# A two-layer fp32 decoder trunk on one core: half of each MLP's first matrix by Strassen's seven products

## The chip, the core and the metric

The kernel runs on one core of a Trainium2 chip. Its engines work at the same time and meet through semaphores: TensorE (PE; its loads of the stationary operand are listed as PEld), VectorE (DVE), ScalarE (ACT), and SyncE (SP), which here only issues DMAs. Each engine takes its instructions in the order in which they stand in the built program. The metric is the device time of one execution in microseconds (us); lower is better.

## The reference

The input has 256 tokens of 2048 features in float32, and everything is computed to float32 accuracy. Layer 0 is differential attention and an MLP, layer 1 a Mamba-2 mixer and an MLP. Only the two MLPs matter here (D_FF is 8192):

```python
def rms_norm(x, gain):
    xf = x.astype(jnp.float32)
    y = xf * lax.rsqrt(jnp.mean(xf * xf, axis=-1, keepdims=True) + EPS)
    return (y * gain.astype(jnp.float32)).astype(x.dtype)
...
def sq_relu_mlp(h, w1, w2):
    return jnp.square(jax.nn.relu(h @ w1)) @ w2
...
        h = h + mix.astype(h.dtype)
        h = h + sq_relu_mlp(rms_norm(h, mlp_norm[i]), mlp_w1[i], mlp_w2[i]).astype(h.dtype)
```

## The kernel before

**Products in two halves.** TensorE multiplies in a rounded type (fp32r). So each float32 operand is split into a high part (ACT's cast) and a low part (what is left, DVE's subtraction), and a product is high x high + low x high + high x low. Weights come from memory as units of 128 x 1024 (512 KB), one DMA each on SP's queue into the tile raw (6 buffers, `load`, L169). `split_weights` (L147) makes wh on ACT (L152) and wl on DVE (L153), with 4 buffers each.

**Two forms of a product.** In the *wide* form (`sub_block`, L156) a 128 x 128 block of weights is stationary, and the activations of all 256 tokens move past it, high and low side by side: 512 columns for wh (L162) and 256 columns for wl (L166). A unit is 8 blocks, so 8 + 8 matmuls. The result stands with features on partitions. In the *token* form (`token_block`, L202) 128 tokens of an activation are stationary and 512 weights move. A unit is 12 matmuls of 512 columns (L216, L218), and the result stands with tokens on partitions.

**The MLP** (`mlp`, L475) goes in four quarters q of 2048 hidden features. A quarter has two stages. The first (W1) makes 16 hidden blocks of 128 features in 8 calls of `wide_pair` (L180), 4 units each. Behind each call `add_sums` (L196) brings the two halves of a PSUM bank together (ACT copy L199, DVE add L200), L485 makes the squared ReLU, and `split_pair` (L227) makes high and low parts (L230, L231). The second (W2) multiplies these with four column blocks of the second matrix (`token_block`, 8 units each), and L490 adds the result, scaled by the token's norm, to h. The eight input tiles xs of the first quarter come from `norm_input` (L250): TensorE transposes h (L259), and `x_parts` (L235) scales and splits (L240 on ACT, L241 on DVE). They are made while the last quarter of the attention's (or the mixer's) output matrix is still being multiplied; `residual` (L282) updates h there (L284).

**Order.** The Python code writes instructions in a nominal order. Generators in `side` are advanced at fixed places (`side.tick()`) and put small work between the matmuls. Behind that a scheduler of the build puts each engine's instructions into their final order. PSUM has 8 banks: 4 for pp (L96), 4 for small results (L97, tags aux and aux1).

Of the kernel before, what the change touches and what calls it, by code (L numbers as in the profile page):

```python
# [12 lines left out]
F32 = mybir.dt.float32  # L13
# [75 lines left out]
def trunk_kernel(ctx: ExitStack, tc: tile.TileContext, x, xt, par, rope, qk, wv, wo, w10, w20, win, wdt, wout, w11, w21, out):  # L89
# [6 lines left out]
    ps = ctx.enter_context(tc.tile_pool(name="ps_mm", bufs=4, space=PSUM))  # L96
    ps_ax = ctx.enter_context(tc.tile_pool(name="ps_ax", bufs=3, space=PSUM))  # L97
# [71 lines left out]
    def load(src, n=1):  # L169

        raw = wp.tile([P, 1024], F32, tag="raw", bufs=6, name="raw")
        w = 1024 // n
        for i in range(n):
            nc.sync.dma_start(out=raw[:, i * w:(i + 1) * w], in_=src[:, i * w:(i + 1) * w])
        return raw

    def bank():
        return ps.tile([P, 2, T], F32, tag="mm", name="pp")
# [23 lines left out]
    def token_block(src, j, acts):  # L202

        pp = [bank().rearrange("p a b -> p (a b)") for _ in range(2)]
        n = src.shape[0]
        for s in range(n):
            w = split_weights(load(src[s, j]))
# [13 lines left out]
        return pp  # L221

# [64 lines left out]

    xs = []
# [23 lines left out]
    with tc.tile_pool(name="att", bufs=1) as ap:  # L312
# [139 lines left out]
        for hd in range(NH):  # L452
# [20 lines left out]


    def mlp(xs, w1, w2, pool, after):  # L475
        r2 = const.tile([P, 2], F32, tag="r2", bufs=2, name="r2")
        for q in range(4):
            hid = []
            for j in range(8):
                r = pool.tile([P, 2, T], F32, tag="relu", bufs=2, name="relu")  # L480
                add_sums(r, wide_pair(w1, 16 * q + 2 * j, xs))
                if q == 0 and j == 1:
                    norm_mean()
                    V.reciprocal(out=r2, in_=ms)
                V.scalar_tensor_tensor(out=r, in0=r, scalar=0.0, in1=r, op0=ALU.max, op1=ALU.mult)  # L485
                hid += split_pair(r)
            for j in range(4):
                pp = token_block(w2[8 * q:8 * q + 8], j, hid)
# [270 lines left out]
def _blocks(w, order=None):  # L759
# [5 lines left out]
    return _units(b)  # L765

# [71 lines left out]
```

## Time and profile before

| What | us |
| --- | --- |
| median of 3 runs (2512.38 to 2512.57) | 2512.4 |
| the profiled execution's own time | 2510.96 |
| its span (first to last instruction) | 2509.2 |
| PE busy in the span | 2493.1 |
| DVE busy | 1668.7 |
| ACT busy | 1310.0 |

The busy time of an engine is the time in which at least one of its instructions ran. Instructions that follow each other overlap a little at their ends, on PE by almost half of a short one: what a chain of them costs is read from the distance of their starts and not from one's duration. A stretch of the span with the engines' busy times in it shows which of them has room there.

### The profile page before, as it was taken

How to read it: one execution, taken by the hardware profiler on the slowest of the kernel's cores; microseconds unless marked ns; L12 is line 12 of the kernel's file. 1: busy time of each engine (PE TensorE's matmuls, PEld its weight loads, DVE VectorE, ACT ScalarE, POOL GpSimd, SP SyncE). 2: the span in 40 equal slices, each digit the busy share in tenths (PEclk: the TensorE clock that was granted, in tenths of full speed). 3: DMA queues.
4: the chain of work that ended last, by engine and by line, in shares of the span. 5: the costliest groups of instructions: out<-in, count | busy, mean ns of one | idle time of the engine just before them, and what ended most of it. 6: DMA issues, size and time to landing. Idle time of an engine off the chain costs nothing.

```text
span 2509.2 us, 33804 instructions
## 1 busy us (share of the span) xinstructions
PE 2493.1 (99%) x13038; PEld 2122.0 (85%) x13038; DVE 1668.7 (67%) x2158; ACT 1310.0 (52%) x1919; POOL 1.2 (0%) x8
## 2 busy tenths in 40 slices
PE   8999999999999999999999999999999999999999
PEld 6888888888888888888888888888888888888887
DVE  7888876655555556558886887887665565555554
ACT  6656655434434434456776575674544443443443
POOL 0000000000000000000000000000000000000000
PEclk9999999999999999999999999999999999999999
DMA  8445555555555565556655556455555555656564
GB/s 276 163 157 181 167 176 183 187 193 193 187 193 191 187 199 187 190 179 207 196 186 195 175 188 207 159 186 187 184 190 193 192 186 193 193 188 193 189 197 139
DMA packets 131122, 471.26 MB, mean 188 GB/s; under 512 B 14640, under 2 KB 14832, under 8 KB 130960
## 3 DMA queue, kind: packets, MB, share of 16 engines
q1 hardware_dynamic: 127152, 458.28, 56.1%
q10 hardware_dynamic: 3808, 10.81, 1.3%
q8 instruction: 102, 1.67, 0.3%
q14 instruction: 60, 0.49, 0.1%
HBM read 466.88 MB, written 2.16 MB: 187 GB/s over the span
## 4 chain that ended last, share of the span: by engine, by line
PE 99%; DMA 1%; SPq 0%; issue 0%; DVE 0%; ACT 0%; DVEq 0%
PE pp L162 35%; PE pp L216 28%; PE pp L166 18%; PE pp L218 14%; PE aux L650 1%; PE aux L135 0%; PE aux L397 0%; PE aux L259 0%; DMA raw<-in_qk 0%; PE aux L620 0%; PE aux L651 0%; PE aux L426 0%; DMA xf<-in_x 0%; PE aux L427 0%; PE aux L607 0%; PE aux L420 0%
## 5 line engine op out<-in xcount | busy, mean ns | idle before, releaser
L153 DVE TENSOR_TENSOR wl<-raw,wh 128x1024 fp32r<-128x1024 f32 (+1 forms) x867 | 1057.2, 1222 | 711.0 <-ACT wh L152 704.8
L152 ACT CAST wh<-raw 128x1024 fp32r<-128x1024 f32 (+1 forms) x867 | 908.1, 1049 | 1074.1 <-PE pp L218 507.0
L162 PE MATMUL pp<-act,wh 128*128 128x512 f32 x3856 | 979.3, 394 | 11.8 <-DVE act L241 11.8
L162 PEld LDWEIGHTS pp<-act,wh 128*128 128x128 f32 x3856 | 693.0, 189 | 138.1 <-ACT wh L152 11.1
L216 PE MATMUL pp<-wh,act 128*128 128x512 f32 x1536 | 601.3, 391 | 0.0
L218 PE MATMUL pp<-wh,act 128*128 128x512 f32 x1536 | 599.0, 390 | 0.0
L166 PEld LDWEIGHTS pp<-act,wl 128*128 128x128 f32 x3856 | 524.6, 191 | 37.7 <-issue 1.7
L166 PE MATMUL pp<-act,wl 128*128 128x256 f32 x3856 | 540.8, 283 | 0.0
L216 PE MATMUL pp<-wl,act 128*128 128x512 f32 x1536 | 413.4, 391 | 0.0
L216 PEld LDWEIGHTS pp<-wh,act 128*128 128x128 f32 x1536 | 288.5, 188 | 60.2 <-issue 1.0
L218 PEld LDWEIGHTS pp<-wh,act 128*128 128x128 f32 x1536 | 288.8, 188 | 58.1
L216 PEld LDWEIGHTS pp<-wl,act 128*128 128x128 f32 x1536 | 286.6, 188 | 59.9 <-issue 1.0
L575 DVE SCALAR_TENSOR_TENSOR cy<-u,cwb,cy 128x256 f32<-128x256 f32 x144 | 62.5, 480 | 21.3 <-ACT cy L573 21.2
L490 DVE SCALAR_TENSOR_TENSOR h<-pp,r,h 128x512 f32<-128x512 f32 x64 | 45.1, 747 | 43.0 <-PE pp L216 43.0
L200 DVE TENSOR_TENSOR relu<-pp,relu 128x256 f32<-128x256 f32 x128 | 53.5, 418 | 0.0
L199 ACT COPY relu<-pp 128x256 f32<-128x256 f32 x128 | 46.9, 367 | 0.0
L485 DVE SCALAR_TENSOR_TENSOR relu<-relu 128x512 f32<-128x512 f32 x64 | 44.3, 692 | 2.2
L635 ACT ACTIVATE m<-ab,acol 128x128 f32<-128x128 f32 x128 | 41.6, 391 | 6.7 <-PE aux L651 6.7
L284 DVE TENSOR_TENSOR h<-pp,h 128x512 f32<-128x512 f32 x48 | 31.0, 685 | 19.7 <-PE pp L216 19.7
L231 DVE TENSOR_TENSOR act<-relu,act 128x512 fp32r<-128x512 f32 x64 | 43.9, 686 | 0.0
L230 ACT CAST act<-relu 128x512 fp32r<-128x512 f32 x64 | 39.2, 613 | 0.0
L240 ACT ACTIVATE act<-aux,pa 128x256 fp32r<-128x256 f32 x48 | 21.6, 472 | 12.4 <-DVE act L241 9.4
(175 smaller groups left out, 954.0 us busy)
## 6 DMA issues: line engine op xcount, KB each, us to landing
raw<-in_w SPq DMA_DIRECT2D x512, 512.0 KB, 4.0
raw<-in_win SPq DMA_DIRECT2D x160, 512.0 KB, 3.5
raw<-in_wout SPq DMA_DIRECT2D x64, 512.0 KB, 3.5
raw<-in_qk SPq DMA_DIRECT2D x63, 512.0 KB, 4.2
raw<-in_wv SPq DMA_DIRECT2D x32, 512.0 KB, 3.3
raw<-in_wo SPq DMA_DIRECT2D x32, 512.0 KB, 3.5
ab<-dram_a ACTq DMA_DIRECT2D x16, 512.0 KB, 5.1
xf<-in_x SPq DMA_DIRECT2D x8, 256.0 KB, 6.6
```

Of the source, the lines that this page charges most:

```text
L152: S.copy(out=wh[:, s], in_=raw[:, s])
L153: V.tensor_tensor(out=wl[:, s], in0=raw[:, s], in1=wh[:, s].bitcast(F32), op=ALU.subtract)
L162: PE.matmul(acc, lhsT=wh[:, k * P:(k + 1) * P], rhs=acts[k0 + k], start=(start and k == 0), stop=False)
L166: PE.matmul(acc[:, 0, :], lhsT=wl[:, k * P:(k + 1) * P], rhs=acts[k0 + k][:, 0, :], start=False, stop=(stop and k == 7))
L199: S.copy(out=dst[:, t, :], in_=pp[t][:, 1, :])
L200: V.tensor_tensor(out=dst[:, t, :], in0=pp[t][:, 0, :], in1=dst[:, t, :], op=ALU.add)
L216: PE.matmul(pp[t], lhsT=act[:, 0, tok], rhs=m, start=(s + i + k == 0), stop=(s == n - 1 and i + k == 2))
L218: PE.matmul(pp[t], lhsT=act[:, 1, tok], rhs=m, start=False, stop=False)
L231: V.tensor_tensor(out=t[:, :, 1, :], in0=src, in1=t[:, :, 0, :].bitcast(F32), op=ALU.subtract)
L485: V.scalar_tensor_tensor(out=r, in0=r, scalar=0.0, in1=r, op0=ALU.max, op1=ALU.mult)
L490: V.scalar_tensor_tensor(out=h[:, t, cols(j)], in0=pp[t], scalar=r2[:, t:t + 1], in1=h[:, t, cols(j)], op0=ALU.mult, op1=ALU.add)
L575: V.scalar_tensor_tensor(out=y[:, i, :], in0=u[:, i, k:k + T], scalar=cwb[:, w + k:w + k + 1], in1=y[:, i, :], op0=ALU.mult, op1=ALU.add)
```

## The change

In each quarter, half of the first matrix (8 of the 16 hidden blocks, 1024 features) is multiplied in the token form by Strassen's method in Winograd's variant. Tokens, inner dimension and features are each cut in two, and the 8 products of the halves become 7 products of sums. The other half stays in the wide form.

- `seven` handles 256 of the 2048 inner features. It loads four weight blocks of 128 x 512 (1 MB, two DMAs L513 and L514, into the tile raw7 with 2 buffers), makes three sums of them on DVE (L529, two blocks in one instruction of 1024; L531 and L532, 512 each), splits all seven blocks (three casts and subtractions of 1024 and one of 512, L522 and L523), and issues 7 x 3 matmuls of 512 columns (L536 to L538) into seven PSUM banks, in which the eight calls of a quarter add up. `seven_out` combines the seven banks into the four results (one ACT copy, seven DVE operations of 512).
- `sum_parts` makes the four sums of activations for each pair of inner blocks, once per MLP: two additions of 256, four operations of 128 and a split of 512 on DVE (L492 to L503).
- `hidden` takes the squared ReLU of the result (L569, one DVE instruction of 2048), transposes it on TensorE (16 transposes of 128 x 128 per quarter, L576) and splits it as before (L240). The W2 stage takes the wide form's hidden blocks first.
- In the nominal order a call of `seven` and a `wide_one` (two units) alternate; in the first quarter two `wide_one` stand ahead, and two calls of `seven` stand alone at the end.
- During an MLP all 8 PSUM banks are one pool (7 + 1 in a W1 stage); elsewhere the pools are as before. The weights' high and low parts share a tile w of 4 buffers; raw has 4 buffers instead of 6. The square's unused output is bf16.

The host lays the Strassen half of the weights out as four blocks per call; it does no sums.

```diff
-        wh = wp.tile([P, 1024], F32R, tag="wh", bufs=4, name="wh")
-        wl = wp.tile([P, 1024], F32R, tag="wl", bufs=4, name="wl")
+        w = wp.tile([P, 2, 1024], F32R, tag="w", bufs=4, name="w")
+        wh, wl = w[:, 0, :], w[:, 1, :]
...
-        raw = wp.tile([P, 1024], F32, tag="raw", bufs=6, name="raw")
+        raw = wp.tile([P, 1024], F32, tag="raw", bufs=4, name="raw")
...
+    def seven(pool, src, acts, pp, start, stop):
+        r = pool.tile([P, 7, NB], F32, tag="raw7", bufs=2, name="raw7")
+        nc.sync.dma_start(out=r[:, 0:3, :], in_=src[:, 0:3, :])
+        nc.sync.dma_start(out=r[:, 6, :], in_=src[:, 3, :])
...
+        parts(0, 2)
+
+        V.tensor_tensor(out=r[:, 3:5, :], in0=r[:, 0:2, :], in1=bc(r[:, 6, :], 2), op=ALU.subtract)
+        parts(2, 2)
+        V.tensor_tensor(out=r[:, 5, :], in0=r[:, 1, :], in1=r[:, 3, :], op=ALU.add)
+        V.tensor_tensor(out=r[:, 6, :], in0=r[:, 5, :], in1=r[:, 2, :], op=ALU.subtract)
+        parts(4, 2)
+        parts(6, 1)
+        for n, ((ah, al), (wh, wl)) in enumerate(zip(acts, ws)):
+            PE.matmul(pp[n], lhsT=ah, rhs=wh, start=start, stop=False)
+            PE.matmul(pp[n], lhsT=al, rhs=wh, start=False, stop=False)
+            PE.matmul(pp[n], lhsT=ah, rhs=wl, start=False, stop=stop)
...
+        def hidden(u, hid):
+            V.scalar_tensor_tensor(out=u, in0=u, scalar=0.0, in1=u, op0=ALU.max, op1=ALU.mult)
+            yield from wait(2)
...
+                        PE.transpose(ax[:, f, t * P:(t + 1) * P], uf[:, t, T * j + P * f:T * j + P * f + P], ident)
+                hid += split_pair(ax)
...
-            for j in range(8):
-                r = pool.tile([P, 2, T], F32, tag="relu", bufs=2, name="relu")
-                add_sums(r, wide_pair(w1, 16 * q + 2 * j, xs))
...
+            for j in range(8 + wait_for):
+                if j >= wait_for:
...
+                    seven(pool, w1s[q, i], sas[i], p7, i == 0, i == 7)
+                    if i == 7:
+                        u = seven_out(pool, p7)
+                if j < 8:
...
+                    add_sums(r[:, j % 2:j % 2 + 1], [wide_one(w1, 8 * q + j, xs)])
```

**PE in a W1 stage.** Before, units of the wide form follow each other (two of them here):

```order
L162 MATMUL pp<-act,wh 128x512 x8
L166 MATMUL pp<-act,wl 128x256 x8
L162 MATMUL pp<-act,wh 128x512 x8
L166 MATMUL pp<-act,wl 128x256 x8
L162 MATMUL pp<-act,wh 128x512 x8
```

After, in the second quarter, two wide units (L168 and L172 are their lines now) and then the products of a call of `seven`, three matmuls each; sa is a sum of activations:

```order
L168 MATMUL pp<-act,w 128x512 x8
L172 MATMUL pp<-act,w 128x256 x8
L168 MATMUL pp<-act,w 128x512 x8
L172 MATMUL pp<-act,w 128x256 x8
L536 MATMUL pp<-w,act 128x512
L537 MATMUL pp<-w,act 128x512
L538 MATMUL pp<-w,act 128x512
L536 MATMUL pp<-w,sa 128x512
L537 MATMUL pp<-w,sa 128x512
L538 MATMUL pp<-w,sa 128x512
L536 MATMUL pp<-w,act 128x512
```

What moved: where four wide units stood, there are now two, and 21 matmuls of the token form.

**DVE in a W1 stage.** Before, one call of `wide_pair` (four splits):

```order
L153 TENSOR_TENSOR wl<-raw,wh 128x1024
L231 TENSOR_TENSOR act<-relu,act 128x2x256
L153 TENSOR_TENSOR wl<-raw,wh 128x1024 x2
L200 TENSOR_TENSOR relu<-pp,relu 128x256
L153 TENSOR_TENSOR wl<-raw,wh 128x1024
L200 TENSOR_TENSOR relu<-pp,relu 128x256
L485 SCALAR_TENSOR_TENSOR relu<-relu 128x512
```

After, one step of the second quarter, from one add of a wide block's halves (L206) to the next; raw_5402 and raw_5490 are the weights of this call of `seven` and of the next:

```order
L206 TENSOR_TENSOR relu<-pp,relu 128x256
L603 SCALAR_TENSOR_TENSOR relu<-relu 128x512
L159 TENSOR_TENSOR w<-raw,w 128x1024 x2
L240 TENSOR_TENSOR act<-relu,act 128x2x256
L523 TENSOR_TENSOR w<-raw_5402,w 128x1024 x2
L529 TENSOR_TENSOR raw_5490<-raw_5490 128x1024
L531 TENSOR_TENSOR raw_5490<-raw_5490 128x512
L532 TENSOR_TENSOR raw_5490<-raw_5490 128x512
L523 TENSOR_TENSOR w<-raw_5402,w 128x1024
L523 TENSOR_TENSOR w_5505<-raw_5490,w_5505 128x512
L206 TENSOR_TENSOR relu<-pp,relu 128x256
```

What moved: the next call's sums (L529 to L532) stand among this call's splits. In every second step L603 and L240 are absent, since a squared ReLU takes two wide blocks, and one more L523 stands behind L529 and not ahead of it.

**DVE where the first quarter begins.** Before, the last update of h and the last input tiles, close together:

```order
L284 TENSOR_TENSOR h<-pp,h 128x512 x2
L153 TENSOR_TENSOR wl<-raw,wh 128x1024
L279 TENSOR_REDUCE ms<-ssq 128x2
L280 TENSOR_SCALAR ms<-ms 128x2
L484 RECIPROCAL r_3841<-ms 128x2
L153 TENSOR_TENSOR wl<-raw,wh 128x1024
L241 SCALAR_TENSOR_TENSOR act<-aux,pa,act 128x256 x4
```

After, the end of that stretch (the update of h stands ten rows ahead of it); L250 is the input tile's low part, L492 to L503 are sums of activations, and L523 is the first split of the first call of `seven`:

```order
L602 RECIPROCAL r_3718<-ms 128x2
L492 TENSOR_TENSOR a<-act 128x256 x2
L250 SCALAR_TENSOR_TENSOR act<-aux,pa,act 128x256
L503 TENSOR_TENSOR sa<-asum,sa 128x512
L496 TENSOR_TENSOR asum<-a 128x128
L523 TENSOR_TENSOR w<-raw_3892,w 128x1024
L250 SCALAR_TENSOR_TENSOR act<-aux,pa,act 128x256 x2
L497 TENSOR_TENSOR asum<-asum,a 128x128
L498 TENSOR_TENSOR asum<-a 128x128
L499 TENSOR_TENSOR asum<-a,asum 128x128
L250 SCALAR_TENSOR_TENSOR act<-aux,pa,act 128x256
```

What moved: sums and a weight split stand among the last four input tiles' rows.

## Rows read from the trace of the kernel before

**Rows 1.** The page: busy time of each engine with its share of the span and its instructions, then the shares of the span in the chain of work that ended last, by engine and by line.

```profile
PE 2493.1 (99%) x13038; PEld 2122.0 (85%) x13038; DVE 1668.7 (67%) x2158; ACT 1310.0 (52%) x1919; POOL 1.2 (0%) x8
...
PE 99%; DMA 1%; SPq 0%; issue 0%; DVE 0%; ACT 0%; DVEq 0%
PE pp L162 35%; PE pp L216 28%; PE pp L166 18%; PE pp L218 14%; PE aux L650 1%; PE aux L135 0%; PE aux L397 0%; PE aux L259 0%; DMA raw<-in_qk 0%; PE aux L620 0%; PE aux L651 0%; PE aux L426 0%; DMA xf<-in_x 0%; PE aux L427 0%; PE aux L607 0%; PE aux L420 0%
```

**Rows 2.** The waits of PE, all of them: who waited for whom, us in total, times, the longest.

```profile
PE pp L162 <- DVE act L241: 11.8, 3, 11.1
```

**Rows 3.** Busy times in three stretches: the last of the attention's output matrix, a W1 stage and a W2 stage. Columns: stretch and its length; busy time (and instructions) of PE, PEld, DVE, ACT, POOL; granted clock of TensorE; share of the DMA engines; GB/s.

```profile
365.00:410.00 45.00, 45.00 (x212) 37.38 (x211) 30.20 (x40) 26.18 (x41) 0.00 (x0) 1.00 0.55 179
430.00:498.00 68.00, 68.00 (x390) 59.77 (x389) 42.00 (x49) 31.93 (x44) 0.00 (x0) 1.00 0.58 190
505.00:585.00 80.00, 80.00 (x355) 66.29 (x354) 40.14 (x36) 31.07 (x30) 0.00 (x0) 1.00 0.60 194
```

**Rows 4.** The timeline of PE where a W2 stage ends and a W1 stage begins (start, time from the first start to the last end, instructions); of a W2 unit only the last four matmuls are shown.

```profile
577.62 1.07 PE L216 MATMUL pp<-wl,act 128*128 128x512 f32 x4
...
585.78 1.07 PE L216 MATMUL pp<-wl,act 128*128 128x512 f32 x4
...
588.50 1.12 PE L166 MATMUL pp<-act,wl 128*128 128x256 f32 x8
589.46 2.00 PE L162 MATMUL pp<-act,wh 128*128 128x512 f32 x8
...
597.84 2.00 PE L162 MATMUL pp<-act,wh 128*128 128x512 f32 x8
```

**Rows 5.** The timeline of PE where the first quarter begins, with the transposes L259.

```profile
409.38 1.98 PE L162 MATMUL pp<-act,wh 128*128 128x512 f32 x8
411.20 0.60 PE L259 MATMUL aux<-ident,h 128*128 128x128 f32 x4
411.56 1.19 PE L166 MATMUL pp<-act,wl 128*128 128x256 f32 x8
```

**Rows 6.** Groups of DVE instructions by line: shape and count, busy time and mean ns of one, idle time before them and what ended it.

```profile
L153 DVE TENSOR_TENSOR wl<-raw,wh 128x1024 fp32r<-128x1024 f32 x865 | 1055.9, 1223 | 711.0 <-ACT wh L152 704.8 <-issue 2.3 <-PE pp L166 1.8
...
L200 DVE TENSOR_TENSOR relu<-pp,relu 128x256 f32<-128x256 f32 x128 | 53.5, 418 | 0.0
...
L485 DVE SCALAR_TENSOR_TENSOR relu<-relu 128x512 f32<-128x512 f32 x64 | 44.3, 692 | 2.2
```

**Rows 7.** The timeline of DVE in two busy stretches, one of the mixer and one of the attention.

```profile
1700.91 1.22 DVE L153 TENSOR_TENSOR wl<-raw,wh 128x1024 fp32r<-128x1024 f32 x1
1702.04 0.69 DVE L641 TENSOR_TENSOR m<-m,cb 128x512 f32<-128x512 f32 x1
1702.64 0.42 DVE L200 TENSOR_TENSOR zz<-pp,zz 128x256 f32<-128x256 f32 x1
1702.98 1.22 DVE L153 TENSOR_TENSOR wl<-raw,wh 128x1024 fp32r<-128x1024 f32 x1
...
32.28 0.49 DVE L123 TENSOR_SCALAR dge<-ident,em 128x128 f32<-128x128 f32 x2
...
36.52 2.36 DVE L153 TENSOR_TENSOR wl<-raw,wh 128x1024 fp32r<-128x1024 f32 x2
...
43.24 0.69 DVE L271 SCALAR_TENSOR_TENSOR rs_c<-rs_c,qt 128x512 f32<-128x512 f32 x1
43.97 0.69 DVE L272 SCALAR_TENSOR_TENSOR rs_c<-rs_c,rs_y 128x512 f32<-128x512 f32 x1
```

**Rows 8.** The timeline of DVE where the first quarter begins.

```profile
409.36 1.29 DVE L284 TENSOR_TENSOR h<-pp,h 128x512 f32<-128x512 f32 x2 [1.09 <-PE pp L216]
...
415.01 0.88 DVE L241 SCALAR_TENSOR_TENSOR act<-aux,pa,act 128x256 fp32r<-128x256 f32 x2 [0.15 <-ACT act L240]
```

**Rows 9.** DMA issues: destination and source, queue, count, KB each, median us from issue to landing. First in the W1 stage from 430 to 498 us, then the output's stores over the whole span, then the first 25 us, in which the DMA engines were full.

```profile
raw<-in_w SPq DMA_DIRECT2D x24, 512.0 KB, 3.4
...
out<-h SPq DMA_DIRECT2D x8, 256.0 KB, 2.5
...
raw<-in_qk SPq DMA_DIRECT2D x7, 512.0 KB, 6.9
```

**Rows 10.** One row for ACT's casts of weights, as in rows 6.

```profile
L152 ACT CAST wh<-raw 128x1024 fp32r<-128x1024 f32 x865 | 907.0, 1050 | 1074.1 <-PE pp L218 507.0 <-PE pp L162 341.0 <-issue 209.9
```

More of the change, by code (lines that the diff above doesn't have):

```diff
@@ L88, in trunk_kernel @@
 @with_exitstack
[L89 removed]
+def trunk_kernel(ctx: ExitStack, tc: tile.TileContext, x, xt, par, rope, qk, wv, wo, w10, w10s, w20, win, wdt, wout, w11, w11s, w21, out):
     nc = tc.nc
@@ L221, in token_block, with rng @@
         return pp
+    def rng(src, a, b):
+        return [src[i] for i in range(a, b)]
     def act_pair():
@@ L466, in trunk_kernel @@
         for j in range(4):
-            residual(token_block(wo[0:4], j, sum((heads[i] for i in range(4)), [])), j)
+            residual(token_block(rng(wo, 0, 4), j, sum((heads[i] for i in range(4)), [])), j)
         side.drain()
@@ new lines, in mlp, with sums_of @@
+    def mlp(xs, w1, w1s, w2, pool, after):
+        r2 = const.tile([P, 2], F32, tag="r2", bufs=2, name="r2")
+        sas = []
+        def sums_of():
+            for j in range(KT // 2):
+                while len(xs) < 2 * j + 2:
+                    yield
+                yield from sum_parts(pool, xs[2 * j:2 * j + 2], sas)
+        def hidden(u, hid):
+            V.scalar_tensor_tensor(out=u, in0=u, scalar=0.0, in1=u, op0=ALU.max, op1=ALU.mult)
+            yield from wait(2)
+            uf = u.rearrange("p t a b -> p t (a b)")
+            for j in range(4):
+                ax = aux().rearrange("p (a b) -> p a b", a=2)
+                for f in range(2):
+                    for t in range(2):
+                        PE.transpose(ax[:, f, t * P:(t + 1) * P], uf[:, t, T * j + P * f:T * j + P * f + P], ident)
+                hid += split_pair(ax)
+                yield
+        side.add(sums_of(), slow=True)
@@ L477, in mlp @@
         for q in range(4):
             hid = []
-            for j in range(8):
-                r = pool.tile([P, 2, T], F32, tag="relu", bufs=2, name="relu")
-                add_sums(r, wide_pair(w1, 16 * q + 2 * j, xs))
[L482 to L486, printed above, removed]
+            p7 = None
@@ new lines, in mlp @@
+            wait_for = 2 if q == 0 else 0
+            for j in range(8 + wait_for):
+                if j >= wait_for:
+                    i = j - wait_for
+                    while len(sas) <= i:
+                        side.tick()
+                    if i == 0:
+                        p7 = [bank().rearrange("p a b -> p (a b)") for _ in range(7)]
+                    seven(pool, w1s[q, i], sas[i], p7, i == 0, i == 7)
+                    if i == 7:
+                        u = seven_out(pool, p7)
+                if j < 8:
+                    if j % 2 == 0:
+                        r = pool.tile([P, 2, T], F32, tag="relu2", bufs=1, name="relu")
+                    add_sums(r[:, j % 2:j % 2 + 1], [wide_one(w1, 8 * q + j, xs)])
+                    if j % 2:
+                        if q == 0 and j == 1:
+                            norm_mean()
+                            V.reciprocal(out=r2, in_=ms)
+                        V.scalar_tensor_tensor(out=r, in0=r, scalar=0.0, in1=r, op0=ALU.max, op1=ALU.mult)
+                        hid += split_pair(r)
```

102 lines of the change are left out of this document (85 added, 17 removed).

## The prediction

> **What bounds the kernel now.** I read the page first: PE is busy for 2493.1 of 2509.2 us, and the chain that ended last is PE for 99% of the span [rows 1]. Then PE's waits: one row of 11.8 us, nearly all a single wait of 11.1 us at the start [rows 2]. Then the stretches: PE is busy without a gap in a W1 and a W2 stage at a granted clock of 1.00, so at the 2.4 GHz level, while DVE is busy for 42.0 of 68.0 us in W1 and for 40.1 of 80.0 us in W2 [rows 3]. So the time is what PE's matmuls need. A microsecond less of them is a microsecond won, as long as DVE (62% busy in W1 before) keeps up with what the change puts on it.
>
> **What the change removes and adds on PE.** Three units of W2 take 585.78 - 577.62 = 8.16 us, so a unit of 12 matmuls takes 2.72 us. Three wide units take 597.84 - 589.46 = 8.38 us, so one takes 2.79 us [rows 4]. A quarter loses half of its 32 wide units: 16 x 2.79 = 44.64 us. It gains 8 calls of `seven` with 21 matmuls of the token form each, 21/12 x 2.72 = 4.76 us a call, 38.08 us. That is 6.56 us less per quarter and 52.5 us less over the 8 quarters of both MLPs. Against it stand 16 transposes per quarter: four of them take 411.56 - 411.20 = 0.36 us between their neighbours [rows 5], so 1.44 us per quarter and 11.5 us in all. Net on PE: 52.5 - 11.5 = **41.0 us less**. The rounding of the unit times moves that by some 2 us.
>
> **What it adds on DVE, in a step of W1.** A step is two wide units and a call of `seven`: 2 x 2.79 + 4.76 = 10.34 us on PE. DVE's instructions in it by the built order: six of 1024 elements (two wide splits, three splits of `seven`, L529), one of 256 (L206), three of 512 (L531, L532, the last split), and in every second step two more of 512 (L603, L240). What one costs where DVE is never idle is the distance of starts [rows 7]: 1.13 us for 1024 (1702.04 - 1700.91; the pair at 36.52 gives 2.36 - 1.22 = 1.14), 0.60 for 512 (1702.64 - 1702.04), 0.34 for 256. With 1.14 a step is 6 x 1.14 + 0.34 + 3 x 0.60 = 8.98 us, or 10.18 us with the two more; mean **9.58 us, 93% of PE's 10.34**. An instruction that needs the one just ahead of it starts 0.73 us behind it and not 0.60 (L272 behind L271) [rows 7]; L531 and L532 are such, so some 0.3 us more, still under 10. ACT's share is lower: five casts at 1.05 us [rows 10], one of 512 and the copies, some 7 us. So I take **no loss inside the steps**: PE remains the bound there. The four w buffers allow it: in the slot order the third split of a call waits longest, for the first wide unit behind the call ahead of it, and is then done about 3 us ahead of its matmuls.
>
> By the Trainium skill ("VectorE: DVE Perf Modes", "The DRAIN you can't avoid") a next operation does not start until the pipeline of the last is empty. The starts in rows 7 contradict that for instructions that don't need each other: L641 begins 1.13 us after an L153 of 1.22 us. The same page adds, in its section on two instructions with no wait between them, that one that is not held starts earlier, and with that the trace agrees. By the first rule the sum is the one of the second rival below.
>
> **The weights' way.** raw7 has two buffers, so a call's load can start only when the call two ahead of it is wholly split, and DVE's L529 needs it. Between that last split and the next L529 stand, by the order, L523 (0.60), L206 (0.34), two wide splits (2.28) and one of `seven` (1.14): 4.4 us in the shorter step. A load of 512 KB lands after 3.4 us in W1, and a store of 256 KB after 2.5 us, so 0.9 us per 256 KB and 3.4 + 1.8 = 5.2 us for 1 MB [rows 9] (an estimate). So DVE waits up to 0.8 us there in the shorter steps, which have 10.34 - 8.98 = 1.36 us to spare: nothing for PE. raw's 4 buffers for 6 cost nothing while such loads land in 3.4 us, since four units are 11 us of PE's work in the other stages.
>
> **Where PE may wait.** (a) *The first quarter's start.* Before, the last input tile is done 415.89 - 409.36 = 6.5 us after h's last update [rows 8]. After, the rows of DVE from that update to the last L250 sum up to 8.7 us: 2 splits of 1024 (2.28), 3 of 512 (1.80), 7 of 256 (2.38), and eleven of 128 or less at 0.20 (L123's pair takes 0.49 us, of which the second alone about 0.29) [rows 7]. PE, which now begins with one block instead of two side by side, asks for that tile after some 36 matmuls and 8 transposes, 7.5 us. So it waits for 1.2 us, and a little for ACT ahead of it: I take 2 us per MLP, 4 us. The bounds are 0 and all that the sums of activations cost: 8 x (2 x 0.34 + 4 x 0.20 + 0.60) = 16.6 us per MLP, if nothing covered them; DVE has 45.0 - 30.2 = 14.8 us free in the 45 us ahead [rows 3], which is where the order puts about half of them. (b) *The end of a quarter.* From the last products to L569's end DVE has six operations of 512 (3.6), two splits (2.28) and L569, which does two times 1024 (2.28): 8.2 us, from about 4.2 us into the last call. PE asks for it 13.0 us into that call (4.76, then two wide units and a W2 unit; in the first quarter, three W2 units). Margin 0.6 us. I take 0.5 us per quarter, 4 us, between 0 and 2 us each. (c) *PSUM pools* that begin and end: at most the two updates of h, 1.29 us [rows 8], at each of four changes; the order lets the first matmul take a free bank, so I take 1 us in all, between 0 and 5.
>
> **The sum**, on the profiled execution's own time: 2510.96 - 41.0 + 4 + 4 + 1 = 2479.0. The median of the runs, 2512.4, is 1.4 us above that execution, so the forecast is **2480 us**, 1.3% less. With no wait at all it is 2512.4 - 41.0 = 2471.4, and 3 us less with the rounding: 2468. With the upper ends of (b) and (c) it is 2480 + 12 + 4 = 2496.
>
> **Rivals.**
> 1. *Loads become the bound, and the kernel is slower.* The place is the ring of two raw7 buffers. Last split, load, L529, and on to that call's last split is one loop per step: the load's L, then L529, one or two splits of 1024, L531 and L532: 3 x 1.14 + 1.20 = 4.62 us or 2 x 1.14 + 1.20 = 3.48 us, mean 4.05. It passes PE's 10.34 us when L is over 6.3 us. There are 7 such steps in each of 8 quarters, 56. It eats the gain left (2512 - 2480 = 32 us) at 0.57 us per step, L = 6.9 us, and makes the kernel slower by over 0.2% from L = 7.0 us. For it: 6.9 us is what 512 KB took where the DMA engines were full [rows 9], a load is now twice as large, and SP's queue is in order, so the wide units' loads stand between two such loads. Against it: in W1 the DMA engines are 58% busy [rows 3], and two buffers' loads do not change the bytes. Its price at L = 6.9 + 1.8 = 8.7 us (a full queue and twice the bytes): 56 x (8.7 + 4.05 - 10.34) = 135 us, **2615 us**.
> 2. *DVE becomes the bound in W1.* If instructions did not overlap, a step would be 6 x 1.22 + 0.42 + 4 x 0.69 = 10.50 us by their durations [rows 6, 7], and 0.16 us would be lost in each of 56 steps: 9 us, **2489 us**. For it: every wait of DVE for ACT or PE has the same effect, and 7% of room is little. Against it: rows 7.
> 3. *The sums of activations are not covered.* 2 x (16.6 - 2) = 29 us more: **2509 us**. For it: DVE is busy for two thirds of the stretch ahead. Against it: the order puts them among that stretch's rows and not behind it, and the first calls of `seven` need few.
> 4. *The change doesn't do what it says.* The built order has 21 matmuls per call and 16 transposes per quarter, so I give it nothing.
>
> **How the numbers follow.** Forecast (2468 to 2496, no long wait anywhere): 0.66. Rival 2, about 2489, or a part of rival 1 with L between 6.3 and 6.8: 0.13. Rival 3, 2509, and a part of rival 1 that ends level: 0.07. Rival 1 in full: 0.14. A measurement of this kernel can tell some 0.2% (5 us) from no change. Faster by more than that: 0.66 + 0.13 = 0.79; within it: 0.07; slower: 0.14. The range holds the forecast and rivals 2 and 3 and leaves rival 1 out, 0.14: 2468 to 2510 us.
>
> **What would show it.** In the profile after: L536 to L538 at 0.227 us a matmul (2.72/12), a call in 4.76 us; the quads of L576 at 0.36 us; a W1 step in 10.34 us, with DVE busy for over 90% of it and PE without a gap; waits of PE only near the start of an MLP and at the quarters' ends, some 10 us in all; loads of raw7 landing in about 5 us. What would prove it wrong: DVE's waits for DMA at L529 followed by PE's waits for w (rival 1); PE's waits for w with DVE never idle (rival 2); a long wait of PE for act or sa in the first quarter (rival 3); a granted clock under 1.00 where PE waits, which rows 3 give no price for.

## The result and the profile after

The kernel after takes 2482.7 us (median of 4 runs, 2481.1 to 2483.1), the kernel before 2512.4 us: ratio 0.988, 95% interval 0.986 to 0.990. It is faster by 29.7 us; the forecast was 2480.

The page: busy times, then the chain that ended last, by engine and by line ([rows 1] before).

```profile
PE 2456.4 (99%) x12462; PEld 2070.8 (83%) x12462; DVE 1967.4 (79%) x2558; ACT 1411.4 (57%) x2007; POOL 1.2 (0%) x8
...
PE 96%; DVE 2%; DMA 1%; issue 0%; ACT 0%; ACTq 0%; SPq 0%; DVEq 0%
PE pp L222 27%; PE pp L168 26%; PE pp L172 14%; PE pp L224 13%; PE pp L536 4%; PE pp L537 4%; PE pp L538 4%; DVE w L159 1%; PE aux L774 1%; PE aux L576 1%; PE aux L141 0%; PE aux L408 0%; DMA raw<-in_w11s 0%; DMA h<-in_xt 0%; PE aux L268 0%
```

PE still bounds the kernel, but DVE now has 2% of the chain and DMA loads of `in_w11s` appear in it. PE's waits, all of them (the one row of [rows 2] has become four):

```profile
PE pp L168 <- DVE act L250: 13.0, 2, 12.5
PE aux L268 <- DVE h L293: 3.3, 3, 1.9
PE pp L168 <- DVE h L293: 2.8, 2, 1.6
PE pp L168 <- DVE h L610: 1.4, 1, 1.4
```

The new waits are all for h, so they lie at the ends of the stages ahead of an MLP and of the mixer, and not one is for w or sa, that is, for the weights and the sums of a step. Six steps of the second quarter and the first quarter's W1 stage, in the columns of [rows 3]:

```profile
592.00:654.09 62.09, 62.09 (x320) 53.16 (x319) 59.04 (x67) 38.19 (x46) 0.00 (x0) 1.00 0.55 186
430.00:498.00 68.00, 68.00 (x346) 58.05 (x345) 67.72 (x86) 42.94 (x54) 0.00 (x0) 1.00 0.54 188
```

DVE is busy for 95% of the six steps and for 99.6% of the first quarter's stage (62% before [rows 3]), and PE has no gap in either. PE's timeline ([rows 4, 5] before): a step of W1, from one first wide unit to the next; two quads of transposes in the W2 stage; the two places where PE waits for h on the way into MLP 0 (at 390 and at 414 us).

```profile
592.00 1.98 PE L168 MATMUL pp<-act,w 128*128 128x512 f32 x8
...
602.34 1.98 PE L168 MATMUL pp<-act,w 128*128 128x512 f32 x8
...
672.74 0.60 PE L576 MATMUL aux<-ident,u 128*128 128x128 f32 x4
673.10 0.48 PE L222 MATMUL pp<-w,act 128*128 128x512 f32 x1
673.41 0.40 PE L224 MATMUL pp<-w,act 128*128 128x512 f32 x1
673.64 0.40 PE L222 MATMUL pp<-w,act 128*128 128x512 f32 x1
...
388.04 0.39 PE L224 MATMUL pp<-w,act 128*128 128x512 f32 x1
390.35 0.33 PE L268 MATMUL aux<-ident,h 128*128 128x128 f32 x1 [1.93 <-DVE h L293]
390.95 0.55 PE L268 MATMUL aux<-ident,h 128*128 128x128 f32 x3 [0.27 <-DVE h L293]
...
414.57 2.09 PE L168 MATMUL pp<-act,w 128*128 128x512 f32 x8 [1.58 <-DVE h L293]
```

A step takes 10.34 us, as forecast. A quad takes 0.36 us up to the next matmul (673.10 - 672.74), but that matmul takes 0.31 up to the one behind it (673.41 - 673.10) instead of 0.23 (673.64 - 673.41): a quad costs 0.44. The kernel before has the same behind its transposes, in the row that follows [rows 5]:

```profile
412.59 0.60 PE L259 MATMUL aux<-ident,h 128*128 128x128 f32 x4
```

Where the time went can be told from one mark, the start of the last pair of updates of h in a quarter's W2 stage (L490 before, L610 after). The table gives the distances between marks on DVE's timeline and, in brackets, the difference to the kernel before. "First quarter of MLP 1" runs from the last mark of MLP 0 and so has the mixer in it.

| Kernel | to MLP 0's first mark | next 3 quarters | mixer and first quarter of MLP 1 | last 3 quarters |
| --- | --- | --- | --- | --- |
| before | 586.67 | 532.02 | 856.72 | 529.28 |
| after | 587.21 (+0.54) | 517.80 (-14.22) | 856.72 (0.00) | 515.03 (-14.25) |
| e1 fixed banks | 584.80 (-1.87) | 517.77 | 853.12 (-3.60) | 515.04 |
| e2 no activation sums | 585.85 (-0.82) | 517.79 | 855.82 (-0.90) | 515.03 |
| e3 no weight sums | 583.99 (-2.68) | 517.80 | 856.52 (-0.20) | 515.02 |
| e4 no Strassen | 588.65 (+1.98) | 532.01 | 859.78 (+3.06) | 529.28 |
| e6 DVE + 1024 | 596.78 (+10.11) | 517.80 | 859.06 (+2.34) | 515.01 |
| e8 DVE + 512 | 592.11 (+5.44) | 517.80 | 856.23 (-0.49) | 515.03 |
| e9 sums held back | 583.96 (-2.71) | 517.76 | 852.65 (-4.07) | 515.02 |

Six quarters win 14.22/3 = 4.74 us each. The two stretches with a first quarter in them win nothing: what is missing between the arithmetic on PE and the result was lost there.

What happens at 390 us is seen on DVE and on SP's queue of the kernel after:

```profile
378.66 0.29 DVE L498 TENSOR_TENSOR asum<-a 128x128 f32<-128x128 f32 x1
381.90 1.23 DVE L529 TENSOR_TENSOR raw<-raw 128x1024 f32<-128x1024 f32 x1 [2.94 <-DMA raw<-in_w10s]
...
389.61 1.28 DVE L293 TENSOR_TENSOR h<-pp,h 128x512 f32<-128x512 f32 x2
```

```profile
368.01 0.33 SPq L513 DMA_DIRECT2D raw<-in_w10s  x1
369.08 5.72 SPq L180 DMA_DIRECT2D raw<-in_wo  x3
374.86 0.42 SPq L514 DMA_DIRECT2D raw<-in_w10s  x1
```

The first call's sums (L529) stand on DVE among the splits of the attention's last matrix. L529 needs both loads of the call; the second of them is issued only at 374.86, behind three loads of the attention's matrix in SP's in-order queue, and it lands some 7 us later (381.9 - 374.86), where the median of these loads is 4.7. So DVE stands still for 2.94 us with work behind it, is never idle afterwards, and updates h at 389.61; PE, done with the block at about 388.4, waits 1.93 and 0.27 us for it. Ahead of MLP 1 DVE waits 1.9 us for such loads at L529, and PE 1.1 us for h.

### The profile page after: what moved, and what is told of

Its sections match the earlier page's. It is cut to its first block, busy times and chain, and to the rows that moved or that the text cites. A ratio compares the mean times of both kernels' runs of the same rounds, so it can differ in the third digit from the quotient of the medians.

```text
span 2481.3 us, 33043 instructions
## 1 busy us (share of the span) xinstructions
PE 2456.4 (99%) x12462; PEld 2070.8 (83%) x12462; DVE 1967.4 (79%) x2558; ACT 1411.4 (57%) x2007; POOL 1.2 (0%) x8
## 4 chain that ended last, share of the span: by engine, by line
PE 96%; DVE 2%; DMA 1%; issue 0%; ACT 0%; ACTq 0%; SPq 0%; DVEq 0%
PE pp L222 27%; PE pp L168 26%; PE pp L172 14%; PE pp L224 13%; PE pp L536 4%; PE pp L537 4%; PE pp L538 4%; DVE w L159 1%; PE aux L774 1%; PE aux L576 1%; PE aux L141 0%; PE aux L408 0%; DMA raw<-in_w11s 0%; DMA h<-in_xt 0%; PE aux L268 0%
## 5 line engine op out<-in xcount | busy, mean ns | idle before, releaser
L159 DVE TENSOR_TENSOR w<-raw,w 128x1024 fp32r<-128x1024 f32 (+1 forms) x739 | 896.3, 1220 | 344.8 <-ACT w L158 341.8
L158 ACT CAST w<-raw 128x1024 fp32r<-128x1024 f32 (+1 forms) x739 | 776.2, 1051 | 594.9 <-PE pp L222 451.6
L222 PE MATMUL pp<-w,act 128*128 128x512 f32 x3072 | 962.7, 392 | 0.0
L168 PE MATMUL pp<-act,w 128*128 128x512 f32 x2832 | 721.7, 394 | 17.2 <-DVE act L250 13.0
L222 PEld LDWEIGHTS pp<-w,act 128*128 128x128 f32 x3072 | 574.7, 188 | 118.7 <-issue 2.1
L168 PEld LDWEIGHTS pp<-act,w 128*128 128x128 f32 x2832 | 511.5, 189 | 114.8 <-ACT w L158 17.9
L224 PE MATMUL pp<-w,act 128*128 128x512 f32 x1536 | 598.5, 390 | 0.0
L172 PEld LDWEIGHTS pp<-act,w 128*128 128x128 f32 x2832 | 384.7, 190 | 28.1 <-issue 1.7
L172 PE MATMUL pp<-act,w 128*128 128x256 f32 x2832 | 398.2, 283 | 0.0
L522 ACT CAST w<-raw 128x1024 fp32r<-128x1024 f32 (+1 forms) x256 | 241.3, 946 | 196.4 <-PE pp L172 111.0
L224 PEld LDWEIGHTS pp<-w,act 128*128 128x128 f32 x1536 | 288.6, 188 | 58.0
L523 DVE TENSOR_TENSOR w<-raw,w 128x1024 fp32r<-128x1024 f32 (+1 forms) x256 | 272.2, 1087 | 41.5 <-ACT w L522 38.5
L536 PE MATMUL pp<-w,sa 128*128 128x512 f32 x256 | 99.9, 390 | 0.0
L537 PE MATMUL pp<-w,sa 128*128 128x512 f32 x256 | 99.8, 390 | 0.0
L538 PE MATMUL pp<-w,sa 128*128 128x512 f32 x256 | 99.6, 389 | 0.0
L529 DVE TENSOR_TENSOR raw<-raw 128x1024 f32<-128x1024 f32 x64 | 78.1, 1221 | 6.8 <-DMA raw<-in_w10s 3.8
L537 PE MATMUL pp<-w,act 128*128 128x512 f32 x192 | 75.2, 391 | 0.0
L536 PE MATMUL pp<-w,act 128*128 128x512 f32 x192 | 75.1, 391 | 0.0
L538 PE MATMUL pp<-w,act 128*128 128x512 f32 x192 | 74.7, 389 | 0.0
L536 PEld LDWEIGHTS pp<-w,sa 128*128 128x128 f32 x256 | 48.1, 188 | 10.5
```

The source lines that it names most:

```text
L168: PE.matmul(acc, lhsT=wh[:, k * P:(k + 1) * P], rhs=acts[k0 + k], start=(start and k == 0), stop=False)
L172: PE.matmul(acc[:, 0, :], lhsT=wl[:, k * P:(k + 1) * P], rhs=acts[k0 + k][:, 0, :], start=False, stop=(stop and k == 7))
L222: PE.matmul(pp[t], lhsT=act[:, 0, tok], rhs=m, start=(s + i + k == 0), stop=(s == n - 1 and i + k == 2))
L224: PE.matmul(pp[t], lhsT=act[:, 1, tok], rhs=m, start=False, stop=False)
L522: S.copy(out=w[:, 0], in_=r[:, a:a + n, :])
L523: V.tensor_tensor(out=w[:, 1], in0=r[:, a:a + n, :], in1=w[:, 0].bitcast(F32), op=ALU.subtract)
```

## The experiments

**e1: PSUM banks that keep their roles.** My theory was now: the steps are as forecast, and what is missing was lost where pools change and where DVE is full ahead of each first quarter.

```diff
-        psum["mm"] = stack.enter_context(tc.tile_pool(name="ps_mm", bufs=8 if one else 4, space=PSUM))
-        psum["ax"] = None if one else stack.enter_context(tc.tile_pool(name="ps_ax", bufs=3, space=PSUM))
+        psum["mm"] = stack.enter_context(tc.tile_pool(name="ps_mm", bufs=4, space=PSUM))
+        psum["ax"] = stack.enter_context(tc.tile_pool(name="ps_ax", bufs=3, space=PSUM))
...
-        pp = bank()
+        pp = aux1().rearrange("p (a b) -> p a b", a=2) if one else bank()
...
-                        p7 = [bank().rearrange("p a b -> p (a b)") for _ in range(7)]
+                        p7 = [bank().rearrange("p a b -> p (a b)") for _ in range(4)] + [aux() for _ in range(3)]
...
```

> The eight PSUM banks keep their roles (4 pp, 3 aux, 1 aux1) for the whole kernel, no pool begins or ends; in a W1 stage the seven sums stand in 4 + 3 of them and the wide blocks in the eighth, as many as before. Theory (a pool that begins waits for the last reader of the pool ahead of it, 1.4 to 1.6 us of PE at the start of MLP 0, of the mixer and of MLP 1): 3 to 5 us less than 2482.7, so 2478 to 2480, and these waits of L168 for h are gone from PE's list. Rival (PE would wait at these places anyway, since DVE is late with the last input tile): the waits for h become waits for act, 2481 to 2483.

Measured: 2477.9 us, 4.9 less than after; ratio to before 0.987 (0.985 to 0.988). Three of its four runs took 2477.1 to 2478.3 us, one 2484.0. PE's waits:

```profile
PE pp L168 <- DVE act L250: 13.0, 2, 12.5
PE aux L268 <- DVE h L293: 1.7, 3, 1.0
```

The waits of L168 for h are gone and none took their place. In the kernel after, the first matmul behind a change of pools waited for the last reader of the old pool; with as many banks that keep their roles it waits for nothing, so a bank was free. The theory holds; the rival does not.

Not all of the 4.9 us is the pools. L268's waits for h also fell, from 3.3 to 1.7 us, and the cause is seen on DVE (e1's L525 is L529 of the kernel after) and on PE:

```profile
380.99 1.23 DVE L525 TENSOR_TENSOR raw<-raw 128x1024 f32<-128x1024 f32 x1 [2.02 <-DMA raw<-in_w10s]
...
389.44 0.33 PE L268 MATMUL aux<-ident,h 128*128 128x128 f32 x1 [1.00 <-DVE h L293]
```

DVE's order up to h's update is the same in both, and SP issued the second load at the same time (374.87 for 374.86), but here DVE waited 0.9 us less for its landing (2.02 for 2.94), and PE waited 0.9 us less for h (1.00 for 1.93).

**e4: the change without Strassen** is the counterpart: the MLP of the kernel before, all else kept.

```diff
-                    seven(pool, w1s[q, i], sas[i], p7, i == 0, i == 7)
...
-                    add_sums(r[:, j % 2:j % 2 + 1], [wide_one(w1, 8 * q + j, xs)])
...
+                add_sums(r, wide_pair(w1, 16 * q + 2 * j, xs))
```

> The MLP of the kernel before (wide form for all of W1), with all else of the change kept: PSUM pools that change, raw with 4 buffers, wh and wl in one tile, bf16 square. Theory: the buffers cost nothing and the pool changes up to 4.5 us: 2512.4 to 2517. Rival (raw's 4 buffers or the shared tile cost PE waits in the attention and the mixer): over 2517, with waits of PE for w there.

Measured: 2516.5 us, as its theory had it; ratio to before 1.0017 (1.0008 to 1.0026). PE's waits for h are those at the three pool changes, and there is none for w:

```profile
PE pp L168 <- DVE act L250: 12.7, 2, 12.2
PE pp L168 <- DVE h L293: 2.5, 2, 1.2
PE pp L168 <- DVE h L573: 1.4, 1, 1.4
```

So the pool changes cost about 4 us, the shared w tile and raw's 4 buffers nothing that a wait of PE shows, and the Strassen part by itself is worth 2516.5 - 2482.7 = 33.8 us.

**e2 and e3: sums left out.** e2 leaves out the sums of activations, the products take plain activations; e3 leaves out the sums of weights, the splits take loaded blocks again. Both change what is computed.

```diff
...
-        s1, s2, s3, s4 = ([sa[:, i, n, :] for i in range(2)] for n in range(4))
+        s1, s2, s3, s4 = ([x[n // 2][:, i, n % 2 * P:n % 2 * P + P] for i in range(2)] for n in range(4))
```

```diff
-        V.tensor_tensor(out=r[:, 3:5, :], in0=r[:, 0:2, :], in1=bc(r[:, 6, :], 2), op=ALU.subtract)
-        parts(2, 2)
-        V.tensor_tensor(out=r[:, 5, :], in0=r[:, 1, :], in1=r[:, 3, :], op=ALU.add)
-        V.tensor_tensor(out=r[:, 6, :], in0=r[:, 5, :], in1=r[:, 2, :], op=ALU.subtract)
-        parts(4, 2)
+        parts(1, 2)
+        parts(0, 2)
```

> Leaves out the sums of activations (additions and split, L492 to L503): the products take plain activations, so the result is another; PE's work is the same. Theory (the stretch ahead of each first quarter is late by some 3 us because DVE has no room there): 2 x 3 us less than 2482.7, 2475 to 2479. Rival (the sums are covered, and the first quarters lose their time to the pool changes and the weights' sums alone): within 1.5 us of 2482.7. The prediction's third rival (the sums stand uncovered) would give 2 x 14 to 17 us back: 2449 to 2455.

> Leaves out the sums of weights (L529, L531, L532; the splits take the loaded blocks again), so the result is another; 2.3 us of DVE per call less, PE's work is the same. Theory (PE bounds the steps, DVE's room is enough): nothing in the steps, a little (1 to 3 us) ahead of the first quarters: 2479 to 2482. Rival (DVE's waits cost PE something in the steps): 56 steps x 0.1 us or more, 2477 or less, and the steps on PE shorter than 10.34 us.

Measured: e2 2481.4 us, e3 2480.3 us, 1.3 and 2.4 us less than after. For e3 the theory was right. For e2 the rival was right: the sums of activations are nearly all covered, and my theory of a DVE that is merely full fell with it. In e2's trace DVE still waits 2.95 us for the first load, and PE 1.54 us for h. In e3, where no L529 waits for that load, the wait of L268 for h falls from 3.3 to 0.5 us. The later quarters do not change by 0.05 us in either (table), although e3 takes 2.3 us of DVE's work from each call: inside the steps DVE costs nothing. What was left as the cause is the wait for the load at L529, ahead of queued splits.

**e5: the first sums on GpSimd.** To take that wait out of DVE's queue I gave the first two calls' sums, and the seventh block's split, to the idle GpSimd (on top of e1).

```diff
+        E = G if first else V
...
-        V.tensor_tensor(out=r[:, 3:5, :], in0=r[:, 0:2, :], in1=bc(r[:, 6, :], 2), op=ALU.subtract)
+        E.tensor_tensor(out=r[:, 3:5, :], in0=r[:, 0:2, :], in1=bc(r[:, 6, :], 2), op=ALU.subtract)
...
-                    seven(pool, w1s[q, i], sas[i], p7, i == 0, i == 7)
+                    seven(pool, w1s[q, i], sas[i], p7, i == 0, i == 7, q == 0 and i < 2)
```

> e1_fixed_banks, and in the first two calls of each MLP GpSimd, which is idle, makes the sums of weights and the whole split of the seventh block, so that no instruction of DVE or ACT that waits for these loads stands ahead of the attention's (or the mixer's) own splits and updates of h. Theory (DVE stood still up to 2.9 us for the first load at L529, with the attention's splits queued behind it, and PE then waited for h): PE's waits for h at L268 are gone, 2.5 to 5 us less than e1's 2477.9: 2473 to 2475.5. Rival (DVE is simply full there, the wait for the load costs nothing): 2477 to 2478. Second rival (GpSimd is slow or slows DVE, and the first call waits for it): over 2479.

Measured: 2491.3 us, 13.4 more than e1. The second rival was right. POOL's timeline and DVE's in the same microseconds:

```profile
381.25 2.40 POOL L529 TENSOR_TENSOR raw<-raw 128x1024 f32<-128x1024 f32 x1 [356.35 <-DVE act L250]
383.74 1.35 POOL L531 TENSOR_TENSOR raw<-raw 128x512 f32<-128x512 f32 x1
```

```profile
381.46 2.48 DVE L488 TENSOR_TENSOR a<-act 128x256 f32<-128x256 f32 x1
383.97 1.26 DVE L492 TENSOR_TENSOR asum<-a 128x128 f32<-128x128 f32 x1
```

DVE's additions of 256 (0.42 us elsewhere) and 128 (0.29) each end only when GpSimd's instruction ends. PE then waited 8.6 us for h, and TensorE came back at half clock (stretches of e5 in the columns of [rows 3]):

```profile
397.40:400.00 2.60, 2.42 (x7) 1.87 (x8) 2.60 (x6) 2.15 (x6) 0.60 (x1) 0.50 0.45 173
400.00:402.00 2.00, 2.00 (x8) 1.67 (x7) 1.55 (x4) 1.21 (x4) 0.00 (x0) 0.50 0.73 262
402.00:404.00 2.00, 2.00 (x9) 1.60 (x9) 1.82 (x3) 1.34 (x3) 0.00 (x0) 0.89 0.00 0
```

**e9 and e10: the first sums later on DVE.** The same question without GpSimd: L529 of the first two calls is held, in DVE's order alone, behind the second and third update of h (e9), or the third and fourth (e10).

```diff
...
+            last = V.tensor_tensor(out=h[:, t, cols(j)], in0=pp[t], in1=h[:, t, cols(j)], op=ALU.add)
+        marks.append(last)
...
+        with tc.issue_after(behind.ins) if behind is not None else ExitStack():
+            V.tensor_tensor(out=r[:, 3:5, :], in0=r[:, 0:2, :], in1=bc(r[:, 6, :], 2), op=ALU.subtract)
```

> e1_fixed_banks, and on DVE the first call's L529 of each MLP is held behind the second of the four updates of h, the second call's behind the third (order only, no wait); all other work is the same, GpSimd idle. Theory (in-order DVE stood still at L529 for a load that had not landed, with the attention's splits behind it; by then the load has landed): PE's wait for h at L268 is gone, 1.5 to 4 us less than e1's 2477.9: 2474 to 2476.5. Rival (DVE is simply full ahead of the first quarter, its 2.9 us of idle time there cost nothing): 2477 to 2479.

> As e9, but held behind the third and the fourth (last) update of h: farther from the load, nearer to the first call. Theory: as e9 or, if the first call's splits come late then, up to 3 us more with a wait of PE for w in the first call: 2474 to 2480.

Measured: 2475.13 and 2475.15 us, 2.7 less than e1 (1.4 between the spans of the profiled executions of e1 and e9, and PE's waits at L268 in e1 are 1.7); ratio to before 0.985 (0.984 to 0.987). PE's waits in e9:

```profile
PE pp L168 <- DVE act L250: 13.2, 2, 12.7
```

Only the start-up is left. The amount of work on DVE is that of e1, so the stretch is not too full; what cost it was the place of L529. These two runs move the sums themselves (L529, L531 and L532, 2.3 us) behind h's update together with the wait for the load, and don't tell the two apart. The kernel after against e1 does: with the sums in the same place, 0.9 us less of waiting for the load was 0.9 us less of PE's wait. Both beat the kernel after, by 7.6 us.

**e6 and e8: more work for DVE in each call.** L529 is issued twice (1024 elements more), or one of its blocks once more (512).

```diff
         V.tensor_tensor(out=r[:, 3:5, :], in0=r[:, 0:2, :], in1=bc(r[:, 6, :], 2), op=ALU.subtract)
+        V.tensor_tensor(out=r[:, 3:5, :], in0=r[:, 0:2, :], in1=bc(r[:, 6, :], 2), op=ALU.subtract)
```

> The kernel after, with L529 issued twice in every call (same result): one more DVE instruction of 1024, 1.14 us per step. Theory (DVE needs 9.58 us of PE's 10.34 per step, its instructions overlapping by 0.09 us each): 10.72 us, 0.38 us over, 56 steps: 2482.7 + 21 = 2504 (2495 to 2512), with PE waiting for w in the steps. Rival (DVE's instructions cost their whole durations, 10.5 us before and 11.7 after): over 2540. Second rival (DVE has more room than that): 2483 to 2487.

> The kernel after, with one more DVE instruction of 512 behind L529 in every call (it writes one of its blocks again, same result): 0.60 us per step. Theory: 10.18 us of PE's 10.34 in the mean, the buffers level the longer steps (10.78) with the shorter ones (9.58): 2483 to 2488. Rival (each longer step binds by itself): 28 x 0.44 = 12 us more, 2495.

Measured: e6 2493.9 us (+11.2), e8 2486.4 us (+3.7). e8 lies where expected. e6 is below its theory's 2495 to 2512, and the table shows that the theory is wrong in kind: the later quarters lose nothing at all, in e6 (517.80 and 515.01, as after) or in e8; MLP 0's first quarter loses 9.6 us more than in the kernel after in e6, MLP 1's 2.3. Six later steps of e6:

```profile
601.56:663.64 62.08, 62.08 (x319) 53.14 (x318) 61.49 (x69) 36.83 (x45) 0.00 (x0) 1.00 0.54 183
```

DVE is busy for 99% of them and PE has no gap, but DVE falls behind. The last split and the last matmul of a call, for the third and the eighth call of this quarter:

```profile
609.82 0.68 DVE L523 TENSOR_TENSOR w<-raw,w 128x512 fp32r<-128x512 f32 x1
622.03 0.39 PE L539 MATMUL pp<-w,act 128*128 128x512 f32 x1
...
668.36 1.83 DVE L523 TENSOR_TENSOR w<-raw,w 128x1024 fp32r<-128x1024 f32 x2 [0.47 <-ACT w L522]
673.76 0.39 PE L539 MATMUL pp<-w,act 128*128 128x512 f32 x1
```

DVE is 11.5 us ahead in the third call (622.03 - 610.50) and 3.6 us in the eighth (673.76 - 670.19); in the kernel after it is 14.6 and 14.4. A step in which DVE needs a little more than PE is no loss by itself: it uses up the lead with which DVE enters a W1 stage, and 8 steps are too few to use it all. In MLP 0's first quarter, where DVE also has the sums of activations and comes out of a full stretch, the lead of e6 is under 0.6 us from the third call to the sixth (2.3 to 4.1 in the kernel after): there PE waits 4.9 us for w, 4.1 of them behind ACT's casts (L522). Another part of the 9.6 us is the granted clock, which was 0.50 in two stretches of some 3 us there, each behind waits of PE.

**e7: each load twice.**

```diff
+        nc.sync.dma_start(out=r[:, 0:3, :], in_=src[:, 0:3, :])
+        nc.sync.dma_start(out=r[:, 6, :], in_=src[:, 3, :])
```

> The kernel after, with both loads of every call issued twice into the same tile, the second pair behind the first one's landing. A load takes 4.4 us there, so some 8.8 us until the last has landed. Theory (the prediction's ring: load, then 4.05 us of DVE work, against PE's 10.34; bound from 6.3 us on): 2.5 us over in 56 steps, 2482.7 + 140 = 2623 (2570 to 2680), with DVE waiting for DMA at L529. Rival (the ring has more room, the load can start earlier than behind the last split): under 2540.

Measured: 2522.1 us, 39 more than after; the rival was right. SP's queue and DVE:

```profile
622.30 0.33 SPq L513 DMA_DIRECT2D raw<-in_w10s  x1
...
627.28 0.33 SPq L516 DMA_DIRECT2D raw<-in_w10s  x1
```

```profile
620.46 1.81 DVE L525 TENSOR_TENSOR w<-raw,w 128x1024 fp32r<-128x1024 f32 x2
622.62 1.23 DVE L531 TENSOR_TENSOR raw<-raw 128x1024 f32<-128x1024 f32 x1 [0.35 <-DMA raw<-in_w10s]
...
631.56 1.23 DVE L525 TENSOR_TENSOR w<-raw,w 128x1024 fp32r<-128x1024 f32 x1 [0.26 <-ACT w L524]
633.07 1.23 DVE L531 TENSOR_TENSOR raw<-raw 128x1024 f32<-128x1024 f32 x1 [0.28 <-DMA raw<-in_w10s]
```

From the first issue (622.30) to the sums that use it (633.07) a load now takes over 10 us, and still a step is 633.07 - 622.62 = 10.45 us. The build ordered DVE anew for the longer load: the sums (L531 here) stand behind the last split of the call ahead, not among its splits, so one buffer's loop of load, sums and splits spans two steps. My ring of one step was a property of one order. What a slow load costs in the order of the kernel after was not tried.

**e11: eight plain products** in the same token form, no sums of any kind.

```diff
-        for n, ((ah, al), (wh, wl)) in enumerate(zip(acts, ws)):
+        for n, (k, f) in enumerate(((0, 0), (1, 1), (1, 0), (0, 1))):
+            wh, wl = ws[n]
+            for t in range(2):
+                ah, al = (x[k][:, i, t * P:(t + 1) * P] for i in range(2))
...
```

> The kernel after with the 8 plain products in the place of Strassen's 7, in the same token form: 24 matmuls per call, 4 result banks, no sums of weights, of activations or of results. Theory (PE bounds the steps at 0.2267 us per matmul): 3 x 0.2267 = 0.68 us per call, 64 calls, 43.5 us more than 2482.7, less up to 4 us of the sums ahead of the first quarters (e2, e3): 2522 to 2526. So the token form by itself, against the wide form, is worth 64 x 0.14 - 11.5 = -2.5 us with its transposes, and all of the gain is the eighth product. Rival (steps are bound by DVE or by loads): under 2510.

Measured: 2522.3 us, ratio to before 1.004 (1.003 to 1.005). A step of it:

```profile
596.63 1.98 PE L168 MATMUL pp<-act,w 128*128 128x512 f32 x8
...
607.66 1.98 PE L168 MATMUL pp<-act,w 128*128 128x512 f32 x8
```

11.03 - 10.34 = 0.69 us per call for three matmuls more, as PE's price says. e11 has the pool changes too, so the token form by itself is read against e4, which has them as well: 2522.3 - 2516.5 = 5.8 us. With its transposes it is slower than the wide form by that much: the quads cost 14.1 us (32 of 0.44), and the units win 64 x 0.14 = 9.0 back by the prediction's prices, which leaves 5.1. All of the gain, and some 10 us that it has to make up for, the token form's and the pools', is the eighth product that is not there.

## Why the prediction held, step by step

- **PE bounds the kernel**: right; PE is 96% of the chain of the kernel after, and over 90% in all the others but e7 (74%).
- **A call of 4.76 us, a step of 10.34**: right (4.79 from 426.80 to 431.59 us, 10.34; e11 by its 0.69).
- **The transposes, 11.5 us**: too small. I took the distance of a quad to its neighbour, 0.36, and did not look one row on. In [rows 5] eight short matmuls behind a quad take 412.59 - 411.56 = 1.03 us, where others take 0.95 to 0.96 [rows 4]. With 0.44 for each of 32 quads it is 14.1 us, and 52.5 - 14.1 = 38.4 us is PE's gain: 4.8 per quarter against 4.74 measured in six of them.
- **No loss inside the steps**: right, and with more room than the 7% that I saw. DVE's busy time is 9.84 us per step (59.04 / 6) for a forecast of 9.58; e6 shows that a loss would start only when DVE's lead is used up, and a quarter's 8 steps were too few for that. So the second rival's price, 0.16 us in each of 56 steps, was formed wrongly too. In the 62.1 us of e6's six steps 68 of DVE's instructions start, and their durations sum up to 66.9 us, so they overlap. By the Trainium skill ("VectorE: DVE Perf Modes", "The DRAIN you can't avoid") a next operation waits until the pipeline is empty, and one that is not held starts earlier; the trace agrees with the second.
- **Loads of 5.2 us**: 768 KB landed after a median of 4.4 us and 256 KB after 4.7; in time for the steps. The first rival's price (135 us at a load of 8.7 us) was far too high for a kernel that the build may order anew: e7 paid 39 us with loads of 10.
- **(a) The first quarter's start, 2 us per MLP**: the place and the cause were wrong. I looked for PE's wait at the last input tile and charged the sums of activations; they cost 1.3 us in all (e2). The wait was 24 us ahead of the MLP's first matmul (414.57 - 390.35), at the second of h's last four updates, since L529 stood in DVE's queue ahead of a load that SP's queue held back. It cost 3.3 us by PE's waits at L268 over both MLPs, 2.7 us from e1 to e9. I had seen DVE and SP as in-order queues for the steps, not for the first call.
- **(b) The ends of the quarters, 4 us**: nothing. The six later quarters win 4.74 of 4.8 us, and no row of PE waits there.
- **(c) The PSUM pools, 1 us**: the term that was mis-sized most: 1.58 + 1.25 + 1.4 = 4.2 us by PE's waits for h at L168, one at each of three changes (the prediction counts four). e1's 4.9 us has some of L268's wait in it. I trusted the order, in which the first matmul takes a free bank; a pool that begins waits for the whole pool ahead of it.
- **The sum**: 9 us of waits were forecast, 29.7 of 38.4 us came, so 8.7 us are missing. PE's waits in the profile are 8.7 us longer than before (20.5 for 11.8): 4.2 in (c), 3.3 in (a) and 1.2 at the kernel's start. (The two profiled executions lie only 27.9 us apart, so some 2 us of theirs are in no wait.) With the transposes' 2.6 us the result is 2.3 us more than forecast. The forecast was right because PE's arithmetic carries most of it. That 9 us of waits were forecast and 8.7 found is luck: of the three terms none had its right size, (b) was nothing, (c) four times as long, and (a) had another cause.

The 1.2 us at the start stay open. PE's first wait is 12.5 us in the profile after and 11.1 before [rows 2], 11.7 to 13.5 in all the profiles of changed kernels, e4's too; with one profile of the kernel before I can't say whether that is more than chance.

## What to carry to other kernels

Where one engine bounds all stages, count its instructions: that gives the sign and most of the size. Then look for what is missing at the seams between stages: which pool begins, which instruction of the next stage stands early in an in-order queue, and whether the load that it needs is held by another queue. An engine that needs a few per cent more than the bound in each step is not yet a loss; ask how far ahead it enters the stage, and how many steps there are.

## What I had not expected of the hardware

- A GpSimd addition of 1024 elements (2.40 us) and one of 512 (1.35) held DVE's additions with two SBUF inputs until they ended: 2.48 us for 0.42, 1.26 for 0.29 (e5). Products with an input in PSUM (L250) kept their 0.47. The Trainium skill ("SBUF — State Buffer", "Who interferes with whom") says that a DVE instruction with two SBUF inputs contends with a GpSimd instruction that reads SBUF; the trace agrees, and with it GpSimd is no place for DVE's overflow here.
- After PE's wait of 8.6 us in e5 the granted clock was 0.50, the 1.2 GHz level, from 397.4 to 402 us, with PE at work, and back at 1.00 from 404 us on. In e6 it was also 0.50 behind waits of 1.78 and 0.27 us for h at the same place, and in the kernel after it stayed at 1.00 behind 1.93 and 0.27, so the length of the wait alone did not decide it. Stretches of e6 and of the kernel after in the columns of [rows 3]:

```profile
392.00:394.00 2.00, 2.00 (x8) 1.60 (x8) 1.93 (x5) 1.79 (x3) 0.00 (x0) 0.50 0.64 211
392.00:394.00 2.00, 2.00 (x12) 1.65 (x11) 2.00 (x6) 1.97 (x4) 0.00 (x0) 1.00 0.58 168
```

- The first matmul behind four transposes takes 0.31 us up to the next, and others of 512 columns 0.23.
